# A hybrid encoder block: row ends, folds and the routing softmax issued in pieces, gate loads on ScalarE's queue, gate products one unit ahead

## The chip, the core and the metric

The program runs on one core of a Trainium2 chip. The metric is the device time of one execution in microseconds (us); the time before is the median of three executions. The engines are TensorE (PE for matmuls, PEld for its weight loads), VectorE (DVE), ScalarE (ACT), GpSimd (POOL) and SyncE (SP, which here only issues transfers). Each engine works through its own instruction queue in order, and a transfer that ACT issues stands in ACT's queue between its arithmetic.

## What is computed

One layer over 512 positions of width 2048: a normalisation, one wide input projection, two branches (differential attention and a gated spatial MLP) that are gated, merged and projected, and then PEER, a product-key mixture of 16384 single-neuron experts with 8 heads of 16 chosen experts for each position. Cut from the reference:

```python
proj = h @ w_in[l]                                   # q, k, v, z, gate
merged = g[:, :, 0] * (o_a @ w_branch_a[l]) + g[:, :, 1] * (o_b @ w_branch_b[l])
x = x + merged @ w_out[l]
q = (ht @ w_q).reshape(T, P_HEADS, 2, P_HALF)        # PEER on the normalised x
v1, i1 = lax.top_k(s[:, :, 0], P_TOPK)               # s: scores against the sub-keys
v2, i2 = lax.top_k(s[:, :, 1], P_TOPK)
top, pos = lax.top_k(cand, P_TOPK)                   # cand: sums of the two lists
gate = jax.nn.softmax(top, axis=-1)
act = jax.nn.gelu(einsum('td,tkd->tk', xb, u_emb[ib])) * gb
out = einsum('tk,tkd->td', act, v_emb[ib])
y = rmsnorm(x + out, final_norm)
```

## The kernel before, in words

Every large product is made three times in a split format: a 512 KB block of weights is loaded by SP into `raw` (four buffers), ACT rounds it to `wh` (a CAST), DVE subtracts to get the rest `wl` (line 109), and TensorE multiplies `wh` by the high and low part of the operand and `wl` by the high part. `wh` and `wl` have three buffers each.

The first 128 positions go through the block alone ("early", up to about 470 us of the span). The other 384 follow: attention heads, then `merge(0)` with the first branch, the spatial MLP, `merge(1)`, the output projection, and the query projection of PEER. In `merge` each of 16 units is a gate product of two weight loads, a sigmoid on ACT, a branch product of one load and a product on DVE. Up to here a scheduler orders the instructions of each engine.

PEER is done in two ways. For the first 224 positions (128, then groups of 64 and 32 that are called XG) the rows of the chosen experts are gathered from HBM, 8 KB for each of 128 partitions at a time, by POOL (line 288), and used by one pass of DVE each (lines 267 and 274). These "row sets" are spread over all the dense work by a table of due steps. For the last 288 positions all 16384 experts are computed densely: the U phase multiplies by `uT` (128 units `i` of two weight loads, output `pa`, a Gelu, a write of `ga` to HBM), the V phase multiplies the gated result by `v_tiles` (256 steps of one load, output `pvt`).

From the U phase on the order is written by hand: what a step emits stands in each queue in that order. A step of U or V is one weight load: `weights(k)` emits the load some steps ahead and the split two steps ahead, then come 24 matmuls, then side work. The side work that matters here:

- `route(rtp, gbp, tb)`, a generator run in the U phase for three blocks of positions. It makes the lists of best keys, the softmax (lines 375 to 381), the chosen indices, for `tb == 1` twelve small transfers on ACT's queue (lines 417 and 418), and three transposes `prt` with four ACT copies (lines 420 to 428). Each `yield` names a cost; once for each unit `i` a credit of 1.7 is added, and pieces run while the credit is above zero.
- `gates()`, a generator that builds the gate of every expert and position: `hot` on DVE, `off` and `og` on ACT, small matmuls `pgt`, and a write `g_d<-gs` to HBM from ACT's queue after every 16 positions.
- `load_g(grp)`, line 909, reads one group of eight blocks of those gates back as `vg` (1152 KB in pieces of 512 bytes) on SP's queue, among the `raw` loads. The first is emitted when routing and gates have ended, the second twelve steps later, the others at every 16th step of V from its first on. `gated(u)` multiplies by it on DVE.
- `finish_rows(acc, t0, n)`, line 1025: Square with a sum on ACT, five small operations for the root on DVE and POOL (lines 96 to 103), one pass on DVE, and the transfer to `out` on ACT's queue, all emitted in one step. It is called for the first 128 positions at step 26 of V after an addition on DVE (line 1077), and by `folded(g)` for the two groups after their last row set.
- `fold_rows`, line 1031: four matmuls with the matrix `fold` and four ACT copies that add up the parts of a group, all in one step.

A step's pieces of `route` and `gates` follow its matmuls:

```python
if half == 1 and rgen is not None:
    credit += 0.0 if i < 2 else 1.7
    while credit > 0 and rgen is not None:
        cost = next(rgen, None)
```

Of the kernel before, what the change touches and what calls it, by code (L numbers as in the profile page):

```python
# [19 lines left out]
P = 128  # L20
D = 2048
# [32 lines left out]
def hybrid_block(ctx, tc, x, attn_norm, w_in, diff_lambda, diff_subln, gmlp_norm, gmlp_row, wsT, gmlp_bs,  # L54
# [301 lines left out]
    def route(rtp, gbp, tb):  # L356
        if tb > DIRECT:
# [11 lines left out]
            for h in range(HEADS):  # L369
# [6 lines left out]
                                op=OP.subtract)  # L376
        nc.scalar.activation(gate, gate, AF.Exp)
        gs = small.tile([P, HEADS], F32, name="gs")
# [30 lines left out]
        if tb == 1:  # L409
            ei = rtp.tile([P, SLOTS], I32, name="ei")  # L410
            nc.vector.tensor_copy(ei, ef)
            gf = gate.rearrange("p a b -> p (a b)")
            for g, (t0, n) in enumerate(XG):
                m = XSETS[g]
                for j in range(P // n):
                    to, of = slice(j * n, (j + 1) * n), (slice(t0 - P, t0 - P + n), slice(j * m, (j + 1) * m))
                    nc.scalar.dma_start(xslot_e[g][to, :], ei[of])
                    nc.scalar.dma_start(xslot_g[g][to, :], gf[of])
        pt = pt_tile("prt")
# [267 lines left out]
    def merge(br, pair):  # L687
        with tc.tile_pool(name="gt", bufs=2, reuse_waits="tile") as gt:
            for n in range(KT):
                pg = project(w_in[G0 + KT * br + n], hh, "gate")  # L690
                sg = gt.tile([P, LN], F32, name="sg")
                nc.scalar.activation(sg, pg, AF.Sigmoid)
# [215 lines left out]
    def load_g(grp):  # L908
        if grp < NG:
            gms[grp] = pools["vp"].tile([P, NCH, VG, GCH], F32, name="vg", bufs=2)  # L910
            nc.sync.dma_start(
# [24 lines left out]
    for i in range(NE):  # L936
        ps = pp_tile("pa")[:, :TD]
        for half in range(2):
# [8 lines left out]
            if half == 1 and rgen is not None:  # L947
                credit += 0.0 if i < 2 else 1.7
# [31 lines left out]
    with tc.tile_pool(name="pv", bufs=4, space=PSUM, reuse_waits="tile") as pv_pool, \  # L980
# [44 lines left out]
        def finish_rows(acc, t0, n):  # L1025
            scr = gat.tile([P, D], F32, tag="gat", name="gat")
            r = row_scale(scr, acc)
            nc.vector.scalar_tensor_tensor(scr, acc, r, fgain, op0=OP.mult, op1=OP.mult)
            nc.scalar.dma_start(out[t0:t0 + n, :], scr[:n, :])

        def fold_rows(accx, fold):
            for q in range(4):
# [3 lines left out]
                nc.scalar.copy(accx[:, cs], ps)  # L1036

        def folded(g):
            fold_rows(accx[g], folds[g])
            finish_rows(accx[g], *XG[g])  # L1040

        for step in range(KT * NG):
# [30 lines left out]
            if step == 20:  # L1073
                first = gat.tile([P, D], F32, tag="gat", name="gat")
                nc.scalar.dma_start(first, x1_d[:P, :])
            if step == 26:
                nc.vector.tensor_add(acc0, acc0, first)
                finish_rows(acc0, 0, P)
# [5 lines left out]
        assert eaten[0] == len(items), (eaten, len(items))  # L1084
# [81 lines left out]
```

## Time and profile before

| What | Value |
|---|---|
| median of 3 executions | 3428.65 us (3427.03 to 3431.07) |
| profiled execution, its own time | 3429.19 us |
| its span | 3427.5 us |
| DVE, ACT and POOL busy | 2879.8, 1624.9 and 646.9 us (84%, 47%, 19%) |
| mean granted TensorE clock | 0.977 of 2.4 GHz |
| moved by DMA | 1099.54 MB, mean 321 GB/s |

The profile gives busy time for each engine, and for each group of instructions the idle time of its engine just before it with what ended that idle time. Matmuls overlap, so a stretch is best judged by how many matmuls start in it. The windows view counts them for any stretch and gives the clock that TensorE was granted there, as a share of 2.4 GHz: 0.5 is the lower level of 1.2 GHz. The time of the profiled execution is 0.5 us above the median, and 1.7 us of it lie outside the span.

### The profile page before, as it was taken

The page shows a single profiled execution, that of the slowest core. Times are in us where ns is not written, and L with a number is a line of the kernel's source. Part 1 is how long each engine was busy: PE and PEld are TensorE (multiplying, and loading weights), DVE is VectorE, ACT ScalarE, POOL GpSimd, SP SyncE. Part 2 cuts the span into 40 slices and gives each one's busy share as a digit, 9 for nine tenths or more (in the row PEclk, how much of TensorE's full clock was granted, in tenths as well). Part 3 has the DMA queues.
Part 4 walks back from the last instruction along what each step waited for, and adds up shares of the span by engine and source line. Part 5 has one row for each costly group of instructions (what it writes and reads, how often), then busy time and mean ns, then how long its engine had stood idle before and what let it go on. Part 6 is the DMA issues. An engine that isn't in the chain of part 4 may idle for free. (4 is left out here: it accounts for less than half of the span.)

```text
span 3427.5 us, 53633 instructions
## 1 busy us (share of the span) xinstructions
PE 3250.8 (95%) x20673; PEld 3056.0 (89%) x20673; DVE 2879.8 (84%) x3851; ACT 1624.9 (47%) x2431; POOL 646.9 (19%) x507
## 2 busy tenths in 40 slices
PE   7979899989999999899899999999899999989997
PEld 5757678879989998799889999999898999989997
DVE  7878887888888889899899998777768899979974
ACT  6767634332233233333453788887343333333333
POOL 0000000222232223323223322222221111111100
PEclk9999999999999999899999999999999999999998
DMA  8779843869999999898899999999999999989953
GB/s 314 270 287 354 316 154 99 302 234 360 367 354 344 363 364 415 308 333 317 307 338 348 321 360 378 371 373 378 375 326 336 340 361 360 347 295 364 359 208 129
DMA packets 280784, 1099.54 MB, mean 321 GB/s; under 512 B 28144, under 2 KB 81392, under 8 KB 217744
## 3 DMA queue, kind: packets, MB, share of 16 engines
q1 hardware_dynamic: 189664, 560.14, 45.0%
q0 software_dynamic: 66656, 481.47, 37.1%
q10 hardware_dynamic: 24208, 54.50, 4.3%
q8 instruction: 163, 2.67, 0.3%
q14 instruction: 93, 0.76, 0.1%
HBM read 1048.98 MB, written 46.92 MB: 320 GB/s over the span
## 5 line engine op out<-in xcount | busy, mean ns | idle before, releaser
L109 DVE TENSOR_TENSOR wl<-raw,wh 128x1024 fp32r<-128x1024 f32 x992 | 1204.7, 1221 | 381.7 <-ACT wh L804 244.6
L804 ACT CAST wh<-raw 128x1024 fp32r<-128x1024 f32 x512 | 536.6, 1050 | 809.6 <-PE pvt L1051 329.1
L145 ACT CAST wh<-raw 128x1024 fp32r<-128x1024 f32 x480 | 502.0, 1050 | 686.7 <-PE gate L159 187.9
L160 PE MATMUL pa<-h2H,wl 128*128 128x288 f32 x2048 | 615.5, 301 | 27.0 <-DVE wl L109 26.7
L158 PE MATMUL pa<-h2H,wh 128*128 128x288 f32 x2048 | 616.5, 301 | 15.6 <-ACT wh L804 15.6
L1050 PE MATMUL pvt<-aH,wh 128*128 128x288 f32 x2048 | 612.9, 299 | 12.1 <-ACT wh L804 12.1
L1052 PE MATMUL pvt<-aH,wl 128*128 128x288 f32 x2048 | 607.5, 297 | 6.2 <-DVE wl L109 6.2
L159 PE MATMUL pa<-h2L,wh 128*128 128x288 f32 x2048 | 609.4, 298 | 0.0
L1051 PE MATMUL pvt<-aL,wh 128*128 128x288 f32 x2048 | 606.3, 296 | 0.0
L160 PEld LDWEIGHTS pa<-h2H,wl 128*128 128x128 f32 x2048 | 389.1, 190 | 37.1 <-DVE wl L109 35.5
L158 PEld LDWEIGHTS pa<-h2H,wh 128*128 128x128 f32 x2048 | 389.5, 190 | 16.8 <-ACT wh L804 16.8
L1050 PEld LDWEIGHTS pvt<-aH,wh 128*128 128x128 f32 x2048 | 389.3, 190 | 14.2 <-ACT wh L804 13.5
L1052 PEld LDWEIGHTS pvt<-aH,wl 128*128 128x128 f32 x2048 | 390.2, 191 | 8.7 <-DVE wl L109 8.6
L1051 PEld LDWEIGHTS pvt<-aL,wh 128*128 128x128 f32 x2048 | 390.7, 191 | 0.5 <-issue 0.5
L159 PEld LDWEIGHTS pa<-h2L,wh 128*128 128x128 f32 x2048 | 389.5, 190 | 0.0
L274 DVE SCALAR_TENSOR_TENSOR h2n<-gat,slot_a,h2n 128x2048 f32<-128x2048 f32 x127 | 297.7, 2344 | 5.2 <-DMA gat<-in_v_emb,slot_e 5.2
L288 POOL DMA_INDIRECT gat<-in_v_emb,slot_e x128 | 204.4, 1597 | 484.1 <-DVE wl L109 266.0
L267 DVE SCALAR_TENSOR_TENSOR gat<-gat,h2n 128x2048 f32<-128x2048 f32 x128 | 293.2, 2291 | 0.0
L288 POOL DMA_INDIRECT gat<-in_u_emb,slot_e x128 | 151.9, 1187 | 446.8 <-DVE gat L267 315.5
L288 POOL DMA_INDIRECT gat<-in_u_emb,xslot_e x96 | 146.4, 1525 | 437.1 <-DVE wl L109 423.6
L274 DVE SCALAR_TENSOR_TENSOR accx<-gat,xslot_a,accx 128x2048 f32<-128x2048 f32 x96 | 224.9, 2342 | 1.3 <-DMA gat<-in_v_emb,xslot_e 1.2
L267 DVE SCALAR_TENSOR_TENSOR gat<-gat,score 128x2048 f32<-128x2048 f32 x96 | 219.3, 2284 | 4.7 <-DMA gat<-in_u_emb,xslot_e 4.7
(423 smaller groups left out, 5889.6 us busy)
## 6 DMA issues: line engine op xcount, KB each, us to landing
raw<-in_uT SPq DMA_DIRECT2D x256, 512.0 KB, 8.0
raw<-in_v_tiles SPq DMA_DIRECT2D x256, 512.0 KB, 6.8
raw<-in_e_nat SPq DMA_DIRECT2D x144, 512.0 KB, 5.1
raw<-in_w_nat SPq DMA_DIRECT2D x128, 512.0 KB, 5.9
raw<-in_w_in SPq DMA_DIRECT2D x112, 512.0 KB, 6.9
ga_d<-ga ACTq DMA_DIRECT2D x128, 144.0 KB, 6.7
g_d<-gs ACTq DMA_DIRECT2D x18, 1024.0 KB, 10.1
vg<-g_d SPq DMA_DIRECT2D x16, 1152.0 KB, 13.8
```

The lines of the kernel that those rows point to most:

```text
L109: return nc.vector.tensor_tensor(low, full, high.bitcast(F32), op=OP.subtract)
L145: nc.scalar.copy(hi, raw)
L158: mm(ps, hi[:, k, :], xh[:, k0 + k, c0:c1], start=first and k == 0, stop=False)
L159: mm(ps, hi[:, k, :], xl[:, k0 + k, c0:c1], start=False, stop=False)
L160: got = mm(ps, lo[:, k, :], xh[:, k0 + k, c0:c1], start=False, stop=last and k == 7)
L267: used = nc.vector.scalar_tensor_tensor(row, row, 1.0, h2n if g < 0 else h2x[g], op0=OP.mult, op1=OP.mult, accum_out=a)
L274: used = nc.vector.scalar_tensor_tensor(acc, row, a, acc, op0=OP.mult, op1=OP.add)
L288: got = nc.gpsimd.indirect_dma_start(out=row, out_offset=None, in_=items[i][0], in_offset=bass.IndirectOffsetOnAxis(ap=column(i, slot_e, x ...
L804: nc.scalar.copy(hi, src)
L1050: mm(pv, hi[:, j, :], aH, start=j == 0, stop=False)
L1051: mm(pv, hi[:, j, :], aL, start=False, stop=False)
L1052: mm(pv, lo[:, j, :], aH, start=False, stop=j == VG - 1)
```

## The change

1. `finish_rows` and `fold_rows` become generators. They are kept in a list `ends`, and each step of V runs one piece of each: for a group nothing in the first step, two fold matmuls with their copies, two more, Square, the start of the root, the rest of it and the pass on DVE, a step of nothing, and the transfer. The addition for the first 128 positions is a piece of its own.
2. `route` yields a cost of 1.8 at three more places: before and after the softmax's Exp on ACT, and before the transposes `prt`. The credit for each unit is 1.8 in place of 1.7.
3. `load_g` issues on ACT's queue in place of SP's.
4. `merge` emits the gate product and sigmoid of unit n+1 ahead of the branch product of unit n.

```diff
         nc.vector.tensor_tensor(gate, cv, cv[:, :, 0:1].to_broadcast([P, HEADS, TOPK]),
                                 op=OP.subtract)
+        yield 1.8
         nc.scalar.activation(gate, gate, AF.Exp)
+        yield 1.8
         gs = small.tile([P, HEADS], F32, name="gs")
...
                     nc.scalar.dma_start(xslot_g[g][to, :], gf[of])
+        yield 1.8
         pt = pt_tile("prt")
...
+            def unit(n):
+                sg = gt.tile([P, LN], F32, name="sg")
+                nc.scalar.activation(sg, project(w_in[G0 + KT * br + n], hh, "gate"), AF.Sigmoid)
+                return sg
+
+            ahead = [unit(0)]
             for n in range(KT):
-                pg = project(w_in[G0 + KT * br + n], hh, "gate")
-                sg = gt.tile([P, LN], F32, name="sg")
-                nc.scalar.activation(sg, pg, AF.Sigmoid)
+                if n + 1 < KT:
+                    ahead.append(unit(n + 1))
+                sg = ahead[n]
                 hi, lo = load_split(w_ab[n], br)
...
             gms[grp] = pools["vp"].tile([P, NCH, VG, GCH], F32, name="vg", bufs=2)
-            nc.sync.dma_start(
+            nc.scalar.dma_start(
...
-                credit += 0.0 if i < 2 else 1.7
+                credit += 0.0 if i < 2 else 1.8
...
-        def finish_rows(acc, t0, n):
+        def finish_rows(acc, t0, n, before):
+            for _ in before():
+                yield
             scr = gat.tile([P, D], F32, tag="gat", name="gat")
-            r = row_scale(scr, acc)
-            nc.vector.scalar_tensor_tensor(scr, acc, r, fgain, op0=OP.mult, op1=OP.mult)
+            ss = small.tile([P, 1], F32, name="ss")
+            nc.scalar.activation(scr, acc, AF.Square, accum_out=ss)
+            yield
...
+            nc.vector.tensor_scalar(v, ss, 1.0 / D, EPS, op0=OP.mult, op1=OP.add)
+            nc.gpsimd.tensor_tensor(y, v, mhalf, op=OP.pow)
+            yield
+            nc.vector.tensor_mul(t, y, y)
+            nc.vector.tensor_mul(t, t, v)
+            nc.vector.tensor_scalar(t, t, -0.5, 1.5, op0=OP.mult, op1=OP.add)
+            nc.vector.tensor_mul(y, y, t)
+            nc.vector.scalar_tensor_tensor(scr, acc, y, fgain, op0=OP.mult, op1=OP.mult)
+            yield
+            yield
             nc.scalar.dma_start(out[t0:t0 + n, :], scr[:n, :])
 
+        def add_first():
+            first = gat.tile([P, D], F32, tag="gat", name="gat")
+            nc.scalar.dma_start(first, x1_d[:P, :])
+            for _ in range(5):
+                yield
+            nc.vector.tensor_add(acc0, acc0, first)
+            yield
+
         def fold_rows(accx, fold):
+            yield
             for q in range(4):
...
                 nc.scalar.copy(accx[:, cs], ps)
+                if q % 2:
+                    yield
+
+        ends = []
 
         def folded(g):
-            fold_rows(accx[g], folds[g])
-            finish_rows(accx[g], *XG[g])
+            ends.append(finish_rows(accx[g], *XG[g], lambda: fold_rows(accx[g], folds[g])))
...
             if step == 20:
-                first = gat.tile([P, D], F32, tag="gat", name="gat")
-                nc.scalar.dma_start(first, x1_d[:P, :])
-            if step == 26:
-                nc.vector.tensor_add(acc0, acc0, first)
-                finish_rows(acc0, 0, P)
+                ends.append(finish_rows(acc0, 0, P, add_first))
+            ends[:] = [e for e in ends if next(e, "end") != "end"]
             sparse_step(AT_V + step, folded)
```

Three places in the queues show what moves. The first is ACT's queue in V where the group of 64 ends: `COPY accx<-yps` are the folds' copies, `ACTIVATE gat,ss` the Square, `CAST wh` the rounding of one weight block. Before:

```order
1737 L804 CAST wh<-raw 128x1024 x3
1738 L1036 COPY accx_24162<-yps 128x512 x4
1739 L212 ACTIVATE gat,ss<-accx_24162 128x2048
1740 L1029 DMA out_y<-gat 64x2048
1741 L804 CAST wh<-raw 128x1024
```

Now:

```order
1765 L813 CAST wh<-raw 128x1024
1766 L1070 COPY accx_24162<-yps 128x512 x2
1767 L813 CAST wh<-raw 128x1024
1768 L1070 COPY accx_24162<-yps 128x512 x2
1769 L813 CAST wh<-raw 128x1024
1770 L1039 ACTIVATE gat,ss<-accx_24162 128x2048
1771 L813 CAST wh<-raw 128x1024
1772 L935 CAST aH<-vga 128x288 x2
1773 L813 CAST wh<-raw 128x1024 x3
1774 L920 DMA vg<-g_d 128x18x128
1775 L1054 DMA out_y<-gat 64x2048
```

The casts that stood behind the whole chain now stand between its pieces, and the transfer to `out` stands right behind a load of gates.

The second place is ACT's queue near the end of U, at the first load of gates. There `L905 DMA ga_d<-ga` is the write of a unit's result and `L904` its Gelu:

```order
1564 L875 DMA g_d<-gs 128x2048
1565 L813 CAST wh<-raw 128x1024
1566 L904 ACTIVATE ga<-pa 128x288
1567 L905 DMA ga_d<-ga 128x288
1568 L920 DMA vg<-g_d 128x18x128
1569 L813 CAST wh<-raw 128x1024 x2
1570 L904 ACTIVATE ga<-pa 128x288
1571 L905 DMA ga_d<-ga 128x288
```

Before, `DMA vg<-g_d` stood in SP's queue between `raw` loads; now it follows the last write of gates in ACT's queue, and two casts and a Gelu stand between it and the next write there.

The third place is TensorE's queue in `merge(0)`, at the end of the last attention head: `pt<-ident,s` and `pt<-ident,o` are that head's transposes, `po` its weighted values. Before:

```order
2844 L470 MATMUL po<-vE,aT 128x128
2845 L470 MATMUL po<-vN,aT 128x128 x3
2846 L159 MATMUL gate<-hL,wh 128x384
...
2856 L160 MATMUL gate<-hH,wl 128x384
2857 L196 MATMUL pt<-ident,o 128x128 x3
2858 L158 MATMUL branch<-ab0H,wh 128x384
```

Now:

```order
2853 L160 MATMUL branch<-ab0H,wl 128x384
2854 L196 MATMUL pt<-ident,s 128x128 x4
2855 L473 MATMUL po<-vE,aT 128x128
2856 L473 MATMUL po<-vN,aT 128x128 x3
2857 L196 MATMUL pt<-ident,o 128x128 x3
2858 L158 MATMUL branch<-ab0H,wh 128x384
```

The eleven gate matmuls that stood between `po` and the transposes of `o` now stand further ahead, and the head's last three pieces follow one another.

## Rows read from the trace of the kernel before

**Rows 1.** The page: TensorE's busy time, share of the span, instructions.
```profile
PE 3250.8 (95%) x20673; PEld 3056.0 (89%) x20673; DVE 2879.8 (84%) x3851; ACT 1624.9 (47%) x2431; POOL 646.9 (19%) x507
```

**Rows 2.** Windows: length, busy (count) of PE, PEld, DVE, ACT, POOL; clock, DMA, GB/s.
```profile
740.00:760.00 20.00, 12.72 (x62) 10.87 (x61) 13.57 (x22) 8.21 (x13) 4.64 (x6) 0.77 0.76 262
1670.00:1690.00 20.00, 11.90 (x70) 11.32 (x69) 10.95 (x22) 4.33 (x10) 5.23 (x3) 0.74 0.57 187
1690.00:2010.00 320.00, 298.69 (x2151) 291.32 (x2150) 305.78 (x594) 192.28 (x337) 89.37 (x54) 0.97 0.92 336
2100.00:2200.00 100.00, 100.00 (x770) 100.00 (x769) 77.29 (x75) 86.67 (x167) 23.20 (x17) 1.00 0.98 377
2380.00:2510.00 130.00, 120.01 (x868) 117.92 (x867) 95.17 (x96) 45.90 (x62) 32.68 (x21) 0.97 0.99 373
2540.00:2625.00 85.00, 81.77 (x600) 80.78 (x599) 59.29 (x67) 34.70 (x53) 15.06 (x10) 0.98 0.97 346
2630.00:2650.00 20.00, 13.31 (x81) 12.72 (x80) 15.53 (x21) 7.87 (x9) 2.52 (x3) 0.74 0.77 281
2655.00:2700.00 45.00, 43.01 (x323) 42.31 (x322) 38.22 (x47) 17.26 (x22) 7.47 (x6) 1.00 0.92 329
2700.00:3030.00 330.00, 329.39 (x2495) 328.93 (x2495) 298.61 (x355) 124.46 (x154) 46.80 (x45) 1.00 0.95 357
3030.00:3070.00 40.00, 31.40 (x178) 26.61 (x177) 25.02 (x33) 14.28 (x19) 3.44 (x4) 0.87 0.60 209
3285.00:3315.00 30.00, 25.27 (x137) 21.54 (x136) 17.75 (x26) 11.70 (x16) 0.56 (x1) 0.83 0.40 125
```

**Rows 3.** Timeline, first 128 positions' end: start, length, engine, line, [idle before, releaser].
```profile
2631.62 1.92 ACT L212 ACTIVATE gat<-h2n 128x2048 f32<-128x2048 f32 x1 [7.18 <-DVE h2n L1077]
2635.28 2.35 DVE L1028 SCALAR_TENSOR_TENSOR gat<-h2n,nry,fgain 128x2048 f32<-128x2048 f32 x1
2638.12 2.94 ACT L804 CAST wh<-raw 128x1024 fp32r<-128x1024 f32 x3 [4.50 <-DVE gat L1028]
2639.22 0.61 PE L1050 MATMUL pvt<-aH,wh 128*128 128x288 f32 x1 [6.28 <-ACT wh L804]
```

**Rows 4.** ACT's timeline at the group of 64; the fold matmuls by line.
```profile
3047.33 0.59 ACT L1036 COPY accx<-yps 128x512 f32<-128x512 f32 x1 [9.39 <-PE yps L1035]
3059.24 1.04 ACT L804 CAST wh<-raw 128x1024 fp32r<-128x1024 f32 x1 [4.62 <-DVE gat L1028]
L1035 PE MATMUL yps<-accx,fold 128*128 128x512 f32 x16 | 12.1, 929 | 7.6 <-DVE accx L274 7.6
```

**Rows 5.** Lines view, DVE, 1690 to 2010 us: busy us, mean ns, idle before.
```profile
L109 DVE TENSOR_TENSOR wl<-raw,wh 128x1024 fp32r<-128x1024 f32 x82 | 98.4, 1214 | 4.0 <-ACT wh L804 3.9
L274 DVE SCALAR_TENSOR_TENSOR h2n<-gat,slot_a,h2n 128x2048 f32<-128x2048 f32 x39 | 91.5, 2346 | 3.5 <-DMA gat<-in_v_emb,slot_e 3.5
L267 DVE SCALAR_TENSOR_TENSOR gat<-gat,score 128x2048 f32<-128x2048 f32 x10 | 22.8, 2283 | 0.0
L832 DVE TENSOR_TENSOR hot<-iota_f,idx 128x512 f32<-128x512 f32 x23 | 15.7, 684 | 0.0
```

**Rows 6.** ACT's timeline at the copy behind the twelve small transfers.
```profile
1681.82 0.27 ACT L423 COPY idx<-prt 128x128 f32<-128x128 f32 x1 [14.88 <-DMA xslot_g<-gate]
```

**Rows 7.** SP's and ACT's timeline at the first load of gates; DMA issues by line.
```profile
2390.94 0.39 SPq L911 DMA_DIRECT2D vg<-g_d  x1
2391.49 10.80 SPq L794 DMA_DIRECT2D raw<-in_uT  x2
2413.02 1.04 ACT L804 CAST wh<-raw 128x1024 fp32r<-128x1024 f32 x1 [12.51 <-DMA raw<-in_uT]
vg<-g_d SPq DMA_DIRECT2D x16, 1152.0 KB, 13.8
raw<-in_uT SPq DMA_DIRECT2D x256, 512.0 KB, 8.0
```

**Rows 8.** Waits view of PE: us in total, times, longest.
```profile
PE pt L196 <- DVE o L481: 7.6, 3, 5.8
```

More of the change, by code (lines that the diff above doesn't have):

```diff
@@ L1023, in final_gain @@
                 nc.vector.tensor_mul(ys[b][:c1 - c0, cs], ys[b][:c1 - c0, cs], fgain[:c1 - c0, cs])
-        def finish_rows(acc, t0, n):
+        def finish_rows(acc, t0, n, before):
+            for _ in before():
+                yield
             scr = gat.tile([P, D], F32, tag="gat", name="gat")
-            r = row_scale(scr, acc)
-            nc.vector.scalar_tensor_tensor(scr, acc, r, fgain, op0=OP.mult, op1=OP.mult)
-            nc.scalar.dma_start(out[t0:t0 + n, :], scr[:n, :])
+            ss = small.tile([P, 1], F32, name="ss")
+            nc.scalar.activation(scr, acc, AF.Square, accum_out=ss)
+            yield
+            v = small.tile([P, 1], F32, name="nrv")
+            y = small.tile([P, 1], F32, name="nry")
+            t = small.tile([P, 1], F32, name="nrt")
+            nc.vector.tensor_scalar(v, ss, 1.0 / D, EPS, op0=OP.mult, op1=OP.add)
[8 more added lines that the diff above has]
+            yield
+            nc.scalar.dma_start(out[t0:t0 + n, :], scr[:n, :])
+        def add_first():
[5 more added lines that the diff above has]
+            yield
         def fold_rows(accx, fold):
+            yield
             for q in range(4):
@@ L1083, in hybrid_block @@
                     nc.scalar.dma_start(ys[b][:c1 - c0, :], x1_d[T0 + c0:T0 + c1, :])
-        assert eaten[0] == len(items), (eaten, len(items))
+        assert eaten[0] == len(items) and not ends, (eaten, len(items))
         settle(*before)
```

## The prediction

> **What bounds it now.** I read the page first [rows 1]. TensorE is busy for 95% of the span; DVE follows with 84%, ACT has half of its time free. So TensorE's instruction stream sets the end, and a change is worth what it takes out of TensorE's pauses, together with the slow clock that follows a long pause. The windows view then says where these pauses are [rows 2]. In the quiet stretch from 2700 to 3030 us 2495 matmuls start in 330 us: 0.132 us each at full clock, so a step of 24 costs 3.2 us. From 2100 to 2200 us, with gate products among them, it is 0.130. Multiply a stretch's count by that, take it from the stretch's length, and what is left is lost time:
>
> - 2630 to 2650, end of the first 128 positions: 20 - 81 x 0.132 = 9.3
> - 3030 to 3070, group of 64: 178 started, eight of them fold matmuls. The sixteen folds take 12.1 us in all [rows 4], so 6.0 here: 40 - 170 x 0.132 - 6.0 = 11.5
> - 3285 to 3315, group of 32: 30 - 129 x 0.132 - 6.0 = 6.9
> - 1670 to 1690, the twelve small transfers: 20 - 70 x 0.132 = 10.8
> - 1690 to 2010, routing: 320 - 2151 x 0.130 = 40.4
> - 2380 to 2510, end of U with the first two loads of gates: 130 - 868 x 0.132 = 15.4
> - 2540 to 2625 and 2655 to 2700, the next three loads: 85 - 600 x 0.132 = 5.8 and 45 - 323 x 0.132 = 2.4
> - 740 to 760, start of the first merge: TensorE idle for 20 - 12.7 = 7.3, the clock at 0.77
>
> Timelines then say who is late in each.
>
> **Row ends and folds.** At the first 128 positions ACT waits 7.18 us for DVE's addition, runs Square, waits 4.50 us for DVE's pass, and only then casts the next weights; TensorE stands for 6.28 us [rows 3]. The granted clock of those 20 us is 0.74, so part of them ran at 1.2 GHz [rows 2]. At the group of 64 ACT waits 9.39 us for the fold matmuls and 4.62 us more for the pass [rows 4]. In pieces, casts stand between all of these. A piece may hold ACT for about two steps, 6.3 us, before TensorE runs out of split weights; Square takes 1.92 [rows 3], two copies 1.2 [rows 4]. The sum of the losses is 9.3 + 11.5 + 6.9 = 27.7. The folds' own 12.1 us stay; a fold that no longer follows a pause runs at the full clock, which I put at 3 back, a quarter. Against that, the DVE passes stay: three of 2.35 us and one addition, now beside full-speed matmuls, on an engine that is busy 298.6 of 330 us in the quiet stretch [rows 2]. A step leaves DVE 0.3 us to spare, so a pass takes eight steps to work off and now and then `wl` will be late: 3 us. Result **-28**; bounds -20 (each pass and addition shows in full, some 9 us) to -31.
>
> **Routing.** From 1690 to 2010 us DVE is busy 305.8 of 320 and matmuls need 280: DVE is the bound there. 82 weight blocks pass, so DVE needs 3.73 us a step against 3.42. Without routing it needs (98.4 + 91.5 + 22.8 + 15.7) / 82 = 2.79 [rows 5], so routing is 0.94. The costs yielded sum to 18.3 + 2 x 43.3 = 104.9 for the three blocks, at 1.7 a unit 61.7 units; now 23.7 + 2 x 48.7 = 121.1, at 1.8 67.3 units. The same work lies thinner by 61.7 / 67.3: 0.86 a step, 0.08 less, 6.4 us over 82 steps. The eleven steps added at the end need 2.79 + 0.86 = 3.65 of DVE, about what gates and matmuls need. The two pauses around Exp fall away; no row of mine prices them, so between 0 and the 3.9 us that DVE's splits wait for ACT there [rows 5]; I take 2. Of the 10.8 us at the twelve transfers little goes: ACT's 14.88 us wait [rows 6] is for DVE and for the issues themselves, which stay in one piece; only four short copies move behind a cast, under 1 us. Result **-9**; bounds -3 and -16. Gates end some eight steps later, still some 34 steps before U ends, and the last of their products has 17 steps to be made ready in: no cost.
>
> **Loads of gates.** On SP's queue the first `vg` is issued at 2390.94, the two `raw` issues behind it take 10.80 us, and ACT waits 12.51 us for such a block at 2413 [rows 7]. A step has 3.2 us for a block. On ACT's queue the blocks no longer stand behind 1152 KB in small pieces. In V I expect 6.5 of 8.2 back: the loads follow each other at 16 steps and little else is issued there, though the transfer to `out` of the group of 64 now stands right behind one. At the end of U the DMA engines are 0.99 busy from 2380 to 2510 [rows 2], so the bytes are the limit whatever queue they are in; and each second step ACT issues a write of `ga`, which would be held as SP's issue was, up to 10.80 us, of which 6.3 are covered. I take 5 of 15.4, nearer to nothing than to all because of the 0.99. Result **-11.5**; bounds +8 (two holds of 4.5 on top of what is lost now, nothing gained in V) and -21.
>
> The Trainium skill, "DMA: Bandwidth & Descriptors", "Issuing engines are not separate DMA queues", speaks against this part: transfers of all engines end on the same 16 DMA engines and interleave, and issuing from another engine saves only issue time. By that rule this term is about 0 and the sum 3390 (the first rival). The same page's "Queues, rings and completion order" has each DMA engine take turns between queues, which is how the move could help; the 12.51 us wait agrees that what is behind in one queue waits.
>
> **Merges.** The price is the 7.3 us pause; its longest wait is 5.8 us for the last head's `o` [rows 8]. The listing of TensorE's queue shows that the order does not do what the edit's words say: the second gate product stood there ahead of the last branch matmuls already, with eleven of its matmuls between `po` and the transposes of `o`. Now all of it is ahead and head, `po` and `o` follow each other with nothing between; in DVE's queue two passes leave that chain and move ahead of it. I take **-2**, bounds -7 and +3 (one pass of 2.3 more in the chain). The other 31 units show no wait of note, so nothing there.
>
> **Sum.** 28 + 9 + 11.5 + 2 = 50.5. The profiled execution took 3429.2: 3378.7; the median is 0.5 lower, so **3378 us**. The four half-widths (about 5.5, 6.5, 14.5, 5) taken together as independent give 17 either way: 3361 to 3395.
>
> **Rivals.**
> - *The queue of the gate loads does not matter* (DMA engines at 0.99 for it, the 12.51 us wait against): 3378 + 11.5 = 3390. Chance 0.18.
> - *DVE becomes the bound of V.* It is at 90% in the quiet stretch. If passes that were hidden in ACT's stall now delay `wl` at the slow clock again, half of the 28 is lost: 3392. For it: the 0.3 us of slack. Against: the last group's end has no row sets after it. Chance 0.14.
> - *More than the sum:* routing no longer binds DVE at all (-16) and the end of U gets 10 of its 15.4 back: 3366. Chance 0.10.
> - *Slower: ACT's queue jams.* The `ga` writes stand behind `vg` in one queue, and a Gelu needs the write of two units before landed, some 13 us. On SP the load landed after 13.8 us [rows 7]. If small pieces get few turns beside row sets and weights, it lands later and ACT, and with it every cast, waits for the difference, twice. It eats the whole gain where the two waits pass 25 us each, landing after 38; at 60 us the loss is 2 x 47 and the time 3378 + 94 = 3472. Against: once ACT stands, weights and row sets stop too and leave the DMA engines to `vg`. Chance 0.05.
>
> **How the numbers follow.** The forecast has 0.53. The first two rivals lie inside the range of 3358 to 3403, which adds the third case's lower side and a few us above the second rival for both together; outside are the jam and combinations, about 0.17. A measurement of this kernel tells 0.2%, 6.9 us, from no change: faster by more than that means under 3421.8. All cases but the jam, and a little of several bad ends at once, are below: 0.92. Same 0.03, slower 0.05.
>
> **What would show it.** Right: the stretches that answer to 2630, 3045 and 3295 hold no ACT wait on a DVE pass and no clock below 1; the routing stretch starts more than 2151 matmuls in 320 us with DVE still over 0.93; no cast waits over 8 us for `raw` behind a load of gates; at the merge a pause of some 5 us remains before the transposes of `o`. Wrong: ACT standing at `ga` or its write behind `vg`; DVE's `wl` ending most of TensorE's waits in V; a pause at 1676 that shrinks by more than 2 us would mean that I misread the twelve transfers.

## The result, and the profile after

The changed kernel takes 3391.6 us (median of four executions, 3386.1 to 3396.3) against 3427.8 for the kernel before: a ratio of 0.9893, 95% interval 0.9876 to 0.9911, so 36 us less (31 to 42). Measured a second time (run again, below) it is 0.9903 (0.9888 to 0.9918), 34 us. The prediction was 50.5 less, 3378 us. Its range held the time, which lies 13 us above the forecast.

The profiled execution took 3386.1 us, the fastest of the four; that of before, 3429.2, was a little over its median. The pair of traces shows 43 us and so 7 to 9 more than the medians. I use the traces for where time goes, the medians for how much.

The page of the changed kernel, its first line (it answers to [rows 1]) and its DMA issues (these answer to [rows 7]):

```profile
PE 3224.6 (95%) x20673; PEld 3033.4 (90%) x20673; DVE 2876.8 (85%) x3851; ACT 1625.8 (48%) x2431; POOL 656.0 (19%) x507
...
vg<-g_d ACTq DMA_DIRECT2D x16, 1152.0 KB, 24.7
```

The number of instructions is the same on every engine. A load of gates now takes 24.7 us to land (median of sixteen) where it took 13.8.

Windows of the changed kernel. The rows answer to [rows 2], in its order: merge, twelve transfers, routing, end of U, start of V with a load of gates, the first 128 positions' end, and the ends of the groups of 64 and 32.

```profile
740.00:760.00 20.00, 13.43 (x63) 11.79 (x62) 13.72 (x22) 6.94 (x12) 5.02 (x6) 0.74 0.72 258
1670.00:1690.00 20.00, 12.12 (x88) 11.56 (x88) 8.98 (x10) 2.37 (x3) 4.07 (x3) 0.86 0.74 272
1690.00:2010.00 320.00, 297.13 (x2160) 289.10 (x2161) 308.23 (x593) 181.95 (x316) 94.41 (x56) 0.99 0.93 336
...
2380.00:2510.00 130.00, 119.36 (x870) 117.40 (x870) 94.58 (x95) 53.17 (x78) 36.30 (x23) 0.97 1.00 379
2530.00:2605.00 75.00, 75.00 (x569) 75.00 (x568) 54.93 (x62) 33.69 (x54) 16.29 (x12) 1.00 0.99 354
2605.00:2650.00 45.00, 43.15 (x324) 42.68 (x323) 41.45 (x52) 17.78 (x21) 8.45 (x6) 1.00 0.94 348
...
3005.00:3045.00 40.00, 40.00 (x287) 38.09 (x286) 33.45 (x41) 18.09 (x24) 6.82 (x5) 1.00 0.88 340
3250.00:3280.00 30.00, 30.00 (x212) 28.09 (x212) 21.93 (x29) 13.68 (x18) 0.00 (x0) 1.00 0.58 202
```

In V nearly all lost time is gone, and the clock is 1.00 in each stretch: 45 - 324 x 0.132 = 2.2 us are lost at the first 128 positions' end (9.3 before), and TensorE is busy without a break through both folds. Routing and the end of U stand where they stood: 2160 matmuls in 320 us against 2151 (2115 in the second trace, of again), 870 in 130 against 868. The pause at the twelve transfers has only moved out of its 20 us: over 1670 to 1710, which holds all of it each time, 207 matmuls start before, 218 in the changed kernel and 209 in again.

The same from TensorE's waits in V, from 2535 to 3420 us (line, what it waited for, us in total, times, longest). The kernel before:

```profile
PE pvt L1050 <- ACT wh L804: 12.1, 6, 6.3
PE yps L1035 <- DVE accx L274: 7.6, 2, 5.4
PE pvt L1052 <- DVE wl L109: 6.2, 10, 1.1
PE yps L1009 <- DVE accT L1001: 6.2, 4, 2.0
```

and the changed kernel:

```profile
PE yps L1018 <- DVE accT L1010: 6.2, 4, 2.0
PE pvt L1089 <- DVE wl L109: 3.9, 5, 1.1
```

No wait of TensorE for a cast and none for a fold's input is left; the 6.2 us are the transposes at the very end, which the change leaves alone. ACT at the group of 64 shows how (timeline of ACT, changed kernel; it answers to [rows 4]):

```profile
3029.33 0.59 ACT L1070 COPY accx<-yps 128x512 f32<-128x512 f32 x1 [2.08 <-PE yps L1069]
3030.19 0.59 ACT L1070 COPY accx<-yps 128x512 f32<-128x512 f32 x1 [0.27 <-PE yps L1069]
3030.67 1.05 ACT L813 CAST wh<-raw 128x1024 fp32r<-128x1024 f32 x1
3034.22 0.58 ACT L1070 COPY accx<-yps 128x512 f32<-128x512 f32 x1 [2.49 <-PE yps L1069]
3035.07 0.59 ACT L1070 COPY accx<-yps 128x512 f32<-128x512 f32 x1 [0.27 <-PE yps L1069]
3035.56 1.06 ACT L813 CAST wh<-raw 128x1024 fp32r<-128x1024 f32 x1
3036.50 1.92 ACT L1039 ACTIVATE gat<-accx 128x2048 f32<-128x2048 f32 x1
...
3038.41 1.04 ACT L813 CAST wh<-raw 128x1024 fp32r<-128x1024 f32 x1
```

A cast stands between any two pieces; here the wait of 9.39 us for the folds is now at most 2.49, and that of 4.62 for the pass is gone. Over both groups ACT's waits for fold matmuls fall from 20.3 us to 10.6, the longest to 3.1. At the first 128 positions a part of the wait for the addition is left (ACT, then DVE; it answers to [rows 3]):

```profile
2618.84 1.93 ACT L1039 ACTIVATE gat<-h2n 128x2048 f32<-128x2048 f32 x1 [3.24 <-DMA gat<-in_v_emb,xslot_e]
2616.53 2.28 DVE L1061 TENSOR_TENSOR h2n<-h2n,gat 128x2048 f32<-128x2048 f32 x1
```

The profile puts these 3.24 us down to a transfer, but the addition ended at 2618.81, right before the Square: 3.24 us where it was 7.18, and TensorE waits for no cast there.

### The profile page after: what moved, and what is told of

Read it like the earlier page. It is cut to its first block, busy times and chain, and to the rows that moved or that the text cites. A ratio compares the mean times of both kernels' runs of the same rounds, so it can differ in the third digit from the quotient of the medians.

```text
span 3384.4 us, 53659 instructions
## 1 busy us (share of the span) xinstructions
PE 3224.6 (95%) x20673; PEld 3033.4 (90%) x20673; DVE 2876.8 (85%) x3851; ACT 1625.8 (48%) x2431; POOL 656.0 (19%) x507
## 5 line engine op out<-in xcount | busy, mean ns | idle before, releaser
L160 PEld LDWEIGHTS pa<-h2H,wl 128*128 128x128 f32 x2048 | 386.0, 188 | 41.5 <-DVE wl L109 39.9
L288 POOL DMA_INDIRECT gat<-in_v_emb,xslot_e x96 | 106.6, 1110 | 593.4 <-DVE wl L109 581.8
## 6 DMA issues: line engine op xcount, KB each, us to landing
vg<-g_d ACTq DMA_DIRECT2D x16, 1152.0 KB, 24.7
```

The source lines that it names most:

```text
L160: got = mm(ps, lo[:, k, :], xh[:, k0 + k, c0:c1], start=False, stop=last and k == 7)
L288: got = nc.gpsimd.indirect_dma_start(out=row, out_offset=None, in_=items[i][0], in_offset=bass.IndirectOffsetOnAxis(ap=column(i, slot_e, x ...
```

## The experiments

Two measures occur in the expectations. The *step table* gives the start of TensorE's first matmul of each of the 256 steps of U and of V, read from the trace. *Lost time* is what the intervals between starts of successive matmuls have over the usual interval after the same matmul. Parts of the step table, in us:

```
                      U, 256    V, to the     V, steps    V, steps    V, steps
                      steps     last matmul   24 to 48    144 to 176  224 to 240
before                953.0     877.0         89.6        119.3       64.1
the change            951.1     836.8         78.6        106.5       53.8
again                 954.5     833.6         78.6        105.7       54.2
ends_only             951.7     851.0         84.6        108.7       53.8
loads_only            956.6     863.1         85.1        118.2       62.2
gates_sp              954.0     850.6         86.7        111.3       53.8
u_sp                  954.9     839.9         81.8        105.9       54.2
split_act             947.5     834.0         78.4        104.8       54.2
no_route              948.8     841.7         79.7        105.4       54.2
no_merge              954.6     841.2         80.8        108.1       53.8
pass_whole            958.0     847.4         85.7        107.2       55.1
credit15              942.1     845.9         81.6        107.2       54.2
slots                 945.9     841.5         81.1        106.5       53.8
combo                 933.2     836.8         78.9        104.8       53.8
```

The last three columns hold the ends of the first 128 positions and of the groups of 64 and 32.

**again**: the changed kernel, unaltered.

> The changed kernel once more, to give its own spread and a second trace. The four executions shown lie between 3386 and 3396 us, the profiled one at the lower end. Theory: the spread comes from the two loads of gates at the end of U, where ACT stands for as long as a load takes to drain; then a second trace differs from the first in that stretch (2380 to 2510 us) by some us and nowhere else by over 2. Rival: it is spread over the early part and the routing stretch, where DVE and transfers set the time; then U's end shows the same 15 us of lost time again. Median 3386 to 3396.

Measured: 3390.8 (3387.1 to 3393.9), 34.4 less than the kernel before. The rival is nearer. Between the two traces of the same program steps 0 to 208 of U differ by 5.6 us (778.2 and 783.8), the end of U by 2.2, V by 3.2. Kernels with the same U or V give the spread better: V runs from 833.6 to 841.7 over the six that have the change's (the change, again, u_sp, no_route, no_merge, slots), U from 951.1 to 958.0 over four (the change, again, no_merge, pass_whole). So a difference of less than some 8 us between two single traces says little. The last three columns are steadier: 78.6 to 81.8, 105.4 to 108.1 and 53.8 to 54.2 over the six.

**ends_only**: the kernel before, with `finish_rows`, `fold_rows`, `add_first` and `ends` of the change, and nothing else of it.

> The kernel before with the first part of the change alone: row ends and folds in pieces. Read off the steps of V in the two traces, this part is worth 32 us (9 at the first 128 positions, 13 at the group of 64, 10 at the group of 32). Theory: this is nearly the whole gain, so 32 less than the kernel before, 3396. Rival: part of it is owed to the gates' loads having left SP's queue, which feeds the weights that the pieces stand between; then 20 to 25, 3404 or so.

Measured: 3406.1, ratio 0.9946 (0.9931 to 0.9961): 19 us less (13 to 24). In its trace V is 26 shorter; that execution was the fastest of its six, and the one profiled of the kernel before was above its median, so that this pair differs by 27. The rival's 3404 is nearer than the theory's 3396: the 32 was read from the pair of traces of the whole change, and held work of the loads too.

**gates_sp**: the change with one word put back.

```diff
-            nc.scalar.dma_start(
+            nc.sync.dma_start(
                 gms[grp], g_d[...
```

> The changed kernel with the loads of gates back on SP's queue. Theory: at the end of U the move changed one pause for another of the same size (blocked raw issues before, blocked ACT now, some 15 us of lost time in both), and in V it gained some 6 us; so 4 to 7 us slower than the changed kernel, all of it in the first 50 steps of V. Rival 1, the prediction's term: 11.5 slower. Rival 2: the queue does not matter at all, within 2 us. Rival 3: the jam on ACT costs more than the pause on SP did, and this is faster than the changed kernel.

Measured: 3405.2, ratio 0.9943 (0.9928 to 0.9958): 14.5 slower than the changed kernel. The theory's 4 to 7 is wrong; the queue matters by more than the trace of before let me see. In the traces all of it is in V, where 850.6 stands against 833.6 to 841.7. What returns is seen in ends_only, which has the same loads on SP. SP in the timeline of ends_only, at the fifth load of gates:

```profile
2646.85 1.45 SPq L911 DMA_DIRECT2D vg<-g_d  x1
2650.97 5.08 SPq L794 DMA_DIRECT2D raw<-in_v_tiles  x1
```

and ACT in the same stretch of it:

```profile
2654.78 1.05 ACT L804 CAST wh<-raw 128x1024 fp32r<-128x1024 f32 x1 [2.08 <-PE pvt L1079]
2666.71 1.04 ACT L804 CAST wh<-raw 128x1024 fp32r<-128x1024 f32 x1 [10.87 <-DMA raw<-in_v_tiles]
```

The issue of `raw` behind the load is held for 5.08 us, its block lands 15.6 us after that issue began, 2.8 us behind the load itself, and a cast waits 10.87 us for it. This is not one load alone. Of the 14 loads of V in this trace, the first block behind each is held 1.5 to 7.9 us at its issue (median 4.3) and lands 1.3 to 5.3 us after the load, a median of 12.9 us from its issue. In the changed kernel no such issue takes over 0.33 us, and 13 of the 14 blocks land before the load, with a median of 8.7 us. On ACT's queue the same load is slow to land (24.7 us), and nobody waits for it, since it is wanted 16 steps later. One issue behind a load is held there too, the one that the prediction pointed out, the transfer to `out` of the group of 64 (ACT in the changed kernel):

```profile
3048.89 4.37 ACTq L1054 DMA_DIRECT2D out_y<-gat  x1
```

A cast waits 4.66 us there, and TensorE does not wait.

**loads_only**: the kernel before with that one word alone.

> The kernel before with the third part alone: loads of gates on ACT's queue. In the changed kernel this part is worth 14.5 us (3390.8 against 3405.2 without it). Theory A: pauses cover one another. While TensorE stands for a row end, the raw buffers fill, and the load that comes soon after is met from them; with the ends whole a load on SP's queue therefore cost less (5.8 + 2.4 us of lost time in V in the trace of before), and this part alone is worth only 6 to 8: 3417 to 3419. Rival: the parts simply add, as 14.5 + 19 nearly make the whole 34.4; then 14 to 15: 3410 to 3411.

Measured: 3413.8, ratio 0.9963 (0.9948 to 0.9977): 13 us less (8 to 18). Theory A falls: the parts add. In medians 13.2 + 19.1 = 32.3 of 34.4, in the traces' V 13.9 + 26.0 = 39.9 of 40 to 43.

**u_sp**: `load_g` takes the queue as an argument; the two loads at the end of U go to SP's, those of V to ACT's.

> The changed kernel with the two loads at the end of U back on SP's queue, those of V left on ACT's. Theory: in U the two queues cost the same (lost time of 14.7 in the kernel before, 14.8 and 12.6 in the two traces of the changed kernel; TensorE's waits 10.0 against 10.6 and 7.0), so all of the 14.5 is V's: within 3 us of the changed kernel. Rival: the 14.5 is spread over both; then 5 or more slower.

Measured: 3389.1, ratio 0.9893 (0.9876 to 0.9911): 1.7 from the changed kernel, so the theory holds. Within these few us the whole worth of the queue is V's; at the end of U one pause took another's place. This is ACT there in the changed kernel, at the second load (its timeline):

```profile
2457.29 0.33 ACTq L905 DMA_DIRECT2D ga_d<-ga  x1
2457.64 0.46 ACTq L920 DMA_DIRECT2D vg<-g_d  x1
...
2463.27 10.24 ACTq L905 DMA_DIRECT2D ga_d<-ga  x1
2473.61 1.04 ACT L813 CAST wh<-raw 128x1024 fp32r<-128x1024 f32 x1 [10.37 <-DMA raw<-in_uT]
```

and at the first, right behind it and two units later:

```profile
2417.46 2.00 ACT L813 CAST wh<-raw 128x1024 fp32r<-128x1024 f32 x2 [7.67 <-DMA g_d<-gs]
...
2432.88 1.05 ACT L813 CAST wh<-raw 128x1024 fp32r<-128x1024 f32 x1 [2.91 <-DMA raw<-in_uT]
2437.64 0.41 ACT L904 ACTIVATE ga<-pa 128x288 f32<-128x288 f32 x1 [3.71 <-DMA ga_d<-ga]
```

The issue of the write of `ga` is held for 10.24 us behind the load (9.24 in again), and the casts behind it with it. The profile puts the cast's 10.37 down to `raw`. In the trace the block of this cast landed at 2467.20, so until then there was nothing to cast; from there to 2473.51, when the issue ended, it is the issue that ACT waits for. At the first load the write behind it is held for only 2.75 us, and two units later a Gelu waits 3.71 us for that write to land. ACT's longest stand there is ahead of the load and not behind it: the load has to wait until the last write of gates has landed, and on ACT's queue the casts wait with it, 7.67 us (6.85 in again), though the next block had landed at 2411.20.

**split_act**: each load in six parts of three chunks, one part a step, on ACT's queue.

```diff
+            for c in range(0, NCH, 3):
+                parts.append((gms[grp][:, c:c + 3], g_d[c:c + 3, :, grp * VG:(grp + 1) * VG, :]))
...
+            load_part(nc.scalar)
```

> The changed kernel with each load of gates cut into six transfers of 192 KB, issued on ACT's queue at one step each. Theory: the pause at U's end comes from one transfer of 1152 KB in small pieces filling ACT's queue, so that the write of ga behind it is issued or lands 10 to 18 us late and a Gelu, and with it the casts, wait for it. In six parts a write stands behind 192 KB at most, 3 to 4 us; then 8 to 12 of the 13 to 15 us lost at U's end go: 3379 to 3383. Rival: the bytes are the limit (DMA engines 0.99 busy there), and the loss stays within 3 us of what it was: 3388 to 3394.

Measured: 3382.8, ratio 0.9873 (0.985 to 0.9895): 44 less than before and so within the theory's range, 7 to 10 less than the changed kernel, with intervals that overlap. Of the end of U only part was won: from 2380 to 2510 us 901 matmuls start where 870 did, some 4 us. At the first load ACT still stood (timeline of ACT, with the first four parts):

```profile
2412.99 0.50 ACTq L927 DMA_DIRECT2D vg<-g_d  x1
...
2414.45 0.38 ACTq L927 DMA_DIRECT2D vg<-g_d  x1
...
2419.62 0.45 ACTq L927 DMA_DIRECT2D vg<-g_d  x1
2420.84 1.05 ACT L813 CAST wh<-raw 128x1024 fp32r<-128x1024 f32 x1 [1.63 <-PE pa L159]
2432.81 0.37 ACTq L927 DMA_DIRECT2D vg<-g_d  x1
2433.30 1.04 ACT L813 CAST wh<-raw 128x1024 fp32r<-128x1024 f32 x1 [11.40 <-DMA vg<-g_d]
```

The fourth part waited until the first had landed, at 2432.79. It is not because they go into one tile: the second and the third go into it as well and were issued while the first was under way. The trace has the first and the fourth on one semaphore, the signal of a transfer's landing, and the issue of the fourth waits for it. Parts with semaphores of their own were not tried.

**no_route**: the change without the three yields in `route` and with 1.7 a unit.

> The changed kernel with routing as before (no further yields, 1.7 a unit). Theory: DVE binds the routing stretch by its total work, which is the same, and the lost time there falls only from 54 to 52 us by the changed yields; so 2 to 4 us slower than the changed kernel. Rival, the prediction's term: 9 us slower, as the same work lies thinner. In the step table U's step 208 stands 6.5 us earlier with the changed yields, but gates end 8 steps later, with 8 steps' worth of their matmuls (some 3.7 us) still to come.

Measured: 3389.9, ratio 0.9902 (0.9886 to 0.9918). The changed routing is worth nothing that can be measured; the prediction's 9 us is not there, and neither are the theory's 2 to 4.

**credit15**: the change with 1.5 for 1.8.

> The changed kernel with 1.5 in place of 1.8 for each unit of U. Routing ends some 15 units later; gates end some six units later still in time before V. Theory: the changed routing was worth nothing (3389.9 without it) since 1.8 with three more yields leaves the rate of DVE's work almost as it was, but a rate lower by a sixth does help: DVE's 0.94 us a step of routing falls to 0.83 and the lost time of 52 us in this stretch by 8 to 12: 3379 to 3383. Rival: lost time there comes from bursts (one long piece beside two passes of a row set), which the rate does not change: within 3 us of the changed kernel. Rival on the other side: the second load of gates is now not drained when V starts, and V's first steps wait 10 us or more: 3400.

Measured: 3386.0, ratio 0.9885 (0.9866 to 0.9903): 5 less than the changed kernel, between theory and rival and not clear of it by medians alone. In its trace U is 9 to 12 shorter and V 9 to 12 longer than in the two traces of the change. Of the second rival's 10 us in V's first steps there is little: the first 24 take 78.4 us against 76.2, and the rest of V's difference is hardly more than the spread of V. What the rate does is seen when DVE's work from U's start to the last `prt` is divided by the steps (splits, row sets and `hot` left out, summed from the trace):

```
             last prt   steps   routing on DVE   a step   time of a step
before       2073.8     128     144.1            1.126    3.84
the change   2111.0     140     144.4            1.031    3.79
again        2117.4     140     144.3            1.031    3.83
credit15     2195.2     166     144.7            0.871    3.71
slots        2112.6     142     144.5            1.018    3.72
combo        2160.2     158     144.1            0.912    3.68
```

In slots and combo (both below) the pause at the twelve transfers is gone too, some 10 to 12 us or 0.07 to 0.08 a step, so that only credit15 shows the rate by itself.

**no_merge**: the change with the merges of before.

> The changed kernel with the merges as before. Theory: the pause at the end of the last head was 10.4 us of lost time in the trace of the kernel before and is 9.8 in that of the changed one, so the gate products ahead are worth 0 to 2: 3390 to 3393. Rival: the units of both merges gain a little each, out of sight of the waits, and it is 5 or more slower.

Measured: 3392.2, ratio 0.9898 (0.9882 to 0.9915), 1.4 slower than again by the medians, and by the ratio between the two measurements of the changed kernel: as the theory has it, and far inside the noise.

**pass_whole**: the yields after Square, after the root's start and after the pass taken out.

```diff
             nc.scalar.activation(scr, acc, AF.Square, accum_out=ss)
-            yield
...
             nc.gpsimd.tensor_tensor(y, v, mhalf, op=OP.pow)
-            yield
...
             nc.vector.scalar_tensor_tensor(scr, acc, y, fgain, op0=OP.mult, op1=OP.mult)
-            yield
-            yield
```

> The changed kernel with the last pieces of a row end joined: Square, root, pass on DVE and the transfer to out in one step; the addition and the fold matmuls stay pieces of their own. ACT is then held for Square (1.92) and for the wait until the pass is done (4.50 to 4.62), some 6.5 us. Theory: two split blocks of weights, 6.3 us, cover that, as the prediction has it; then each of the three ends costs 0 to 1.5 and the time is 3391 to 3395. Rival: the cover is smaller than two steps, as the next casts and the wl behind them come only after it (1.05 + 1.22 each); then 3 to 5 an end, 3400 to 3406.

Measured: 3397.5 (3390.9 to 3406.1), ratio 0.991 (0.9893 to 0.9928): not told apart from the changed kernel by time. In the step table the two groups' ends cost some 1 us each, as the theory says, but the first 128 positions' end costs 4 to 7 (85.7 against 78.6 to 81.8). The execution traced here was the slowest of the four, 8.6 above the median. ACT there (timeline):

```profile
2625.62 1.05 ACT L813 CAST wh<-raw 128x1024 fp32r<-128x1024 f32 x1
2630.08 1.91 ACT L1039 ACTIVATE gat<-h2n 128x2048 f32<-128x2048 f32 x1 [3.42 <-DVE h2n L1057]
...
2637.72 0.34 ACTq L1050 DMA_DIRECT2D out_y<-gat  x1
2638.19 2.95 ACT L813 CAST wh<-raw 128x1024 fp32r<-128x1024 f32 x3 [6.10 <-DVE gat L1049]
```

and DVE in between:

```profile
2627.77 2.28 DVE L1057 TENSOR_TENSOR h2n<-h2n,gat 128x2048 f32<-128x2048 f32 x1
2629.97 2.34 DVE L274 SCALAR_TENSOR_TENSOR accx<-gat,xslot_a,accx 128x2048 f32<-128x2048 f32 x1
2632.23 1.21 DVE L109 TENSOR_TENSOR wl<-raw,wh 128x1024 fp32r<-128x1024 f32 x1
...
2635.34 2.35 DVE L1049 SCALAR_TENSOR_TENSOR gat<-h2n,nry,fgain 128x2048 f32<-128x2048 f32 x1
```

ACT is held from 2626.67 to 2638.19, 11.5 us and not 6.5. Of the 5 us more, 3.42 are Square's wait for the addition, which the theory left out; the changed kernel has that wait too (3.24), but casts go on right after its Square. The rest is in the 6.10 behind Square, 4.50 in the kernel before: a row set's pass and a split stand ahead of the root in DVE's queue. With 6.3 covered some 5 are left, and 4 to 7 were lost. That fits a cover of two steps; what one must add up against it is DVE's queue, not the piece.

**slots**: a yield of 1.8 between `ei` and the twelve transfers, and one of 0.9 after each two of them; the yield of 1.8 ahead of the transposes `prt` is taken out, for all three blocks.

> The changed kernel with the largest pause that is left in U in pieces too: a yield between the making of the slots on DVE and the twelve small transfers on ACT, and one of 0.9 after each two of them. Theory: ACT stands there 7.4 us for DVE and 10 us for the issues; in pieces casts stand between, and 7 to 10 of the 10 to 12 us lost from 1674 to 1695 go; gates end eight steps later at no cost: 3381 to 3385. Rival: the row sets of the groups of 64 and 32 that wait for these slots come later and DVE, at 0.95 there, gives the time back: 3388 to 3393.

Measured: 3381.3, ratio 0.9867 (0.9851 to 0.9883): 44 less than the kernel before, 9.5 less than the changed one, as the theory says. The window from 1670 to 1710 us, in again:

```profile
1670.00:1710.00 40.00, 30.14 (x209) 28.99 (x208) 27.50 (x37) 10.43 (x17) 11.00 (x6) 0.87 0.76 266
```

and in slots:

```profile
1670.00:1710.00 40.00, 40.00 (x302) 39.84 (x301) 32.87 (x25) 14.24 (x22) 10.24 (x7) 1.00 0.96 361
```

302 matmuls start where 209 did: 93 x 0.132 = 12.3 us. The whole of U is 5 and 9 us shorter than in the two traces of the change (945.9 against 951.1 and 954.5), and the execution traced here was the slowest of its four. In again ACT had stood here for 17.41 us, first for DVE and then for its own issues.

**combo**: split_act and slots together, with 1.6 a unit in place of 1.8.

> The changed kernel with gates' loads in six parts, the twelve transfers in pieces and 1.6 a unit. Theory: the three add: 8 + 7 to 10 + 3 to 5 less than 3390.8, 3368 to 3373. Rival: gates now end so late in U that the parts of the second load are not in when V starts, and 5 to 10 come back: 3376 to 3382.

Measured: 3367.9 (3363.4 to 3371.1), ratio 0.983 (0.9815 to 0.9845): 57 us less than the kernel before and 23 less than the change, at the lower end of the theory's range. This is the best version found. Nearly all that it adds to the change is in U, which takes 933 us in place of 951 and 955. Its window at the end of U:

```profile
2380.00:2510.00 130.00, 127.34 (x949) 126.64 (x948) 99.74 (x102) 73.07 (x121) 28.43 (x19) 0.99 0.99 377
```

949 matmuls, gates' among them since these now end later, against 870.

## Why the prediction was right, and where it was not

The time lies in the range, the mechanism of the two largest terms is there, and the third term, routing, is not. That the range held is partly luck: it is wide mainly because the bounds of the loads are (+8 and -21), and that width took up two other terms which both fell short.

**Row ends and folds, -28.** The place and the way were right: ACT's waits for the pass are gone, those for the addition and the folds about halved, TensorE waits for no cast there, and the clock is 1.00 through all three. By the trace with the loads on ACT's queue in both (loads_only against again) the three stretches give 6.5 + 12.5 + 8.0 = 27, and 23 to 27 if each of the six kernels with these ends is put in again's place. By medians the part is worth 19 (13 to 24), at the lower bound that the prediction gave; with the loads on ACT's queue in both it is 23 (3413.8 less 3390.8), with what routing and merges give. So the term was about right by the traces and too large by the medians, and I can't say which stretch holds the difference, since only one execution of each run has a trace. One piece of it is plain: the prediction booked the whole 9.3 at the first 128 positions, and 2.2 are still lost there. "A quarter" for the folds' clock was too little: the sixteen keep TensorE busy for 7.5 us and not 12.1 [rows 4], 4.6 less where the prediction put 3. The row of the changed kernel:

```profile
L1069 PE MATMUL yps<-accx,fold 128*128 128x512 f32 x16 | 7.5, 592 | 0.0
```

**Routing, -9.** This step failed: "the same work lies thinner by 61.7 / 67.3: 0.86 a step, 0.08 less, 6.4 us over 82 steps". The thinning came about: DVE's routing work fell from 1.126 to 1.031 us a step, 8% as forecast. The steps followed by half at most: 3.84 us before, 3.79 and 3.83 after, and over all traces 3.84 to 3.88 in the four with the old routing against 3.79 to 3.83 in the seven with the new, some 0.045 of 0.095. Twelve more steps go at that pace instead of the 3.65 of a step with gates alone (3.65 in every trace), 2 us. And what U's step 208 gains is moved, not saved: it comes 4.6 us earlier by the means of those traces (781.1 against 785.7 us from U's start), but 32 gate matmuls, 4.2 us at 0.130, which used to stand ahead of it now stand behind it. The pauses around Exp did fall away (ACT's 5.7 us and DVE's 1.1, over three times each, no longer show), and the 2 us booked for them are not seen in the time either. Over the whole of U there is nothing: 951.1 and 954.5 against 953.0, 951.7 and 956.6 for the three kernels with the old routing, and 948.8 for no_route. Why only a part of DVE's time comes back is open. A coarser change of the same knob (0.871 a step, 3.71 us) does shorten U.

**Loads of gates, -11.5.** The size was right, 13.2 alone and 14.5 within the change, and its split was not: "6.5 of 8.2" in V and "5 of 15.4" at the end of U became some 14 and nothing. At the end of U the mechanism of the slower rival appeared at a small scale: `ga`'s write held for 10.24 us, a Gelu waiting for a write behind `vg`; and, which the prediction did not have, ACT standing 7.67 us for what the load itself waits for. Together they cost what the held `raw` had cost. The first rival, that the queue does not matter, gives 3390, close to the time measured; but its reason is false, as loads_only and gates_sp show. By the rule of the Trainium skill, "DMA: Bandwidth & Descriptors", "Issuing engines are not separate DMA queues", that initiating transfers on several engines saves only the time it takes to issue, usually small, both would show next to nothing. The runs show 13 and 14.5, so the measurement decides. Two things were saved in V: the held issues, 4.3 us at the median load in ends_only, and the place of the weights behind the load, which they now pass. What each is worth was not separated.

**Merges, -2.** Right within what can be seen: no_merge is 1.4 slower by the medians, and a pause of 4.4 us for `o` remains where 5.8 stood [rows 8], as the prediction had it.

**The other rivals.** DVE did not become V's bound: `wl` ends 3.9 us of TensorE's waits there, against 6.2 before. The pause at the twelve transfers did not shrink, as said: TensorE's longest wait for a cast there is 7.9 and 9.2 us in the two traces, 7.7 before. slots shows what it was worth. The sign that routing would start more than 2151 matmuls came in one trace (2160) and failed in the other (2115).

**The sum.** 28 became 19, 9 became 0, 11.5 became 13 and 2 became 1, which is 33; 34 to 36 were measured, in place of 50.5. The routing term and what the ends fell short of are about half of the miss each.

## What to carry to other kernels

A chain of short operations that runs through two engines costs little when each piece stands behind the next tile's work, and a great deal when it is emitted in one step: look for idle time on a half-empty engine that ends at another engine, and put the feeding work in between. Add up the other engine's queue against the cover, not the piece's own time. A large transfer in small pieces belongs on a queue in which nothing urgent is issued behind it, and its own landing time matters only against the step that wants it. What the load itself must wait for holds up that queue as well. Where a stretch is held by an engine that is 95% busy, a saving per step is not a saving in time until the steps are seen to get shorter, and a landmark that comes earlier proves nothing if work has moved behind it.

## What was not expected of the hardware

At the second load of gates ACT's queue took the issue of 1152 KB in 0.46 us, and then held the next issue, of 144 KB and five us later, for 10.24 us (9.24 in again). No arithmetic of ACT ran in that time. At the first load, with the next issue two us later, it was 2.75 (2.33 in again). Why the two differ is open.

The same load lands after 24.7 us on ACT's queue and after 13.8 on the weights' queue, with 1152 KB and the same pieces in both. On the weights' queue the next block of weights landed behind the load at each of 14 loads (ends_only); on two queues it landed ahead of it at 13 of 14 (the changed kernel). That the weights so keep more of the DMA engines fits these numbers; it was not tested apart from the held issues, which alone could explain V's 13 us or part of them.
